# Reading out a bank of the main products ahead of the weights and the other side tasks

## The chip, the cores and the metric

The kernel runs on one core of one Trainium2 chip. The metric is the device time of one execution in microseconds. Shown is the median of several runs; beside them stands one execution that the hardware profiler recorded.

## The reference

A two-layer encoder trunk over 512 tokens of width 1024, in float32. Each layer normalises its input, multiplies it with one wide input projection, feeds the result to a token mixer (dilated window attention in layer 0, grouped attention with rotary positions in layer 1), to an attention into 256 memory tokens and to a gate, and projects the gated heads back:

```python
for i in range(DEPTH):
    h = rmsnorm(x, norm_g[i])
    mem_h = rmsnorm(mem, mem_norm_g[i])
    proj = jnp.einsum('bsd,de->bse', h, w_in)          # w_in_a[0] or w_in_b[0]
    ...
    o_mem = memory_attention(q_mem, mem_h, w_mem_kv[i], mem_qn_g[i], mem_kn_g[i])
    y = jnp.concatenate([o_mix, o_mem], axis=-1) * jax.nn.silu(gate)
    x = x + jnp.einsum('bse,ed->bsd', y, w_out[i])
```

## The kernel before

**Exact products in three passes.** Every float32 operand is split into a high part that TensorE takes and a low rest. `mm3` (L147 to L149) issues high x high, high x low, low x high. For the activations the split is made once. For the weights it is made on the way, per tile of 128 x 1024: ScalarE copies the loaded tile `wl` into the high part `wh` (L262), VectorE subtracts it to get the low part `wo` (L272). Both have rings of four buffers.

**Seven products for eight.** A projection is cut into chunks of columns, and each chunk into two by two blocks. `s_chunk` computes it with seven block products in the order of `PRODUCTS`: 12, 11, S1, S2, S4, S3, 22. The sums of weight blocks that this needs are made by VectorE (L231) and by accumulating DMAs that POOL issues (L236, L241, L246). Products with the flag `fresh` begin a new bank of PSUM (`pj`, four banks); S2, S4 and S3 go on in a bank that an earlier product left, after it was read out. Two kinds of generators read the banks: `keep` (ScalarE, L334) copies a bank to SBUF (`sn`), and `add` (VectorE, L344) adds a bank to such a copy, or subtracts, and then goes on with the consumer `ev` of that chunk: norms (L495, L385, L386, L500), rotary positions, transposes, or the gate.

**Slots.** The order of instructions is written by hand, there is no scheduler. After each group of matmuls (a slot) `s_chunk` calls three things in this order: `W.advance()`, which traces at most one `wo` (L272), one sum of weights, one `wh` (L262) and the loads (L217) and forces what the next slot needs; then, if the product is complete, `drv.spawn(f(...), d)` for the generators that read it; then `drv.tick()`, which advances every generator of the queue `urgent` that is due, then those of `bulk` (the attention pipelines), and last the functions of `after`, such as the low parts of transposed probabilities (`lo`, L636 and L1308). With `d` of 2 or 3 a readout is traced one or two slots behind the end of its product, behind that slot's `wo`, sum and `wh`, and at its place among the other generators.

A chunk of layer 0's heads (`head_chunk`) has 512 columns per block, two banks per product and two slots per product; the chunks of layer 1 and the gates have 256, one bank and one slot. The sequence is: a chunk for the values of layer 0, the keys and values of the memory (`mem_kv`, through the plainer `chunk`), eight heads and three gate chunks of layer 0, the output projection (`out_proj`, with operands `y` that `prep_y` makes at L736, L752 to L762), then the same for layer 1, whose attention (`attn_b`: `sb`, `pb`, `ptb`, `pbT`, `ob`) and memory attention (`mem_attn`: `sm`, `pm`, `pmt`, `pmT`, `om`) run as pipelines between the slots.

Of the kernel before, what the change touches and what calls it, by code (L numbers as in the profile page):

```python
# [39 lines left out]
class Driver:  # L40
# [5 lines left out]
    def __init__(self):  # L46
        self.slot = 0
        self.urgent = []
        self.bulk = []
        self.after = []  # L50
        self.first = []

    def spawn(self, gen, delay=0):
        self.urgent.append([self.slot + delay, gen])
# [46 lines left out]
        self.after = []  # L101

    def drain(self):
        while self.urgent or self.bulk or self.first:
            self.tick(ACTIVE)


# [1 line left out]
def trunk_kernel(ctx: ExitStack, tc: tile.TileContext, x, mem, wall, norm_g, mem_norm_g, gcol,  # L109
# [9 lines left out]
    drv = Driver()  # L119
# [7 lines left out]
    def s2(dt=F32, name="s2"):  # L127
        return pool.tile([128, 512], dt, tag="s2", name=name, bufs=NS2)

    def pj(name="pj"):  # L130
        return psum.tile([128, 512], F32, tag="pj", name=name, bufs=4)
# [14 lines left out]
    def mm3(o, lh, ll, rh, rl, start, stop):  # L146
        T.matmul(o, lh, rh, start=start, stop=False, skip_group_check=True)  # L147
        T.matmul(o, lh, rl, start=False, stop=False, skip_group_check=True)  # L148
        T.matmul(o, ll, rh, start=False, stop=stop, skip_group_check=True)  # L149
# [156 lines left out]
    def chunk(units, nb, group, evac):  # L306

        ps = [None] * nb
        for u in range(units):
            w = []  # L310
            for h, l in (W.take(), W.take()):
                w += [(h[:, k * 512:(k + 1) * 512], l[:, k * 512:(k + 1) * 512]) for k in range(2)]
            for b in range(nb):
                if u == 0:
                    ps[b] = pj()
                group(w, u, b, ps[b])
                W.advance()
                if u == units - 1:
                    drv.spawn(evac(b, ps[b]), 2)
                drv.tick()  # L320
# [5 lines left out]
    def s_chunk(n, act, ev, tokens=True, pre=None, half=False):  # L326


        units, per = n // 256, 1024 // n
        bank, snap = [None, None], {}  # L330

        def keep(name, u, b):
            t = snap[name, u] = s2(name="sn")
            A.copy(t, b)  # L334
            yield 1
            if name == "s3":
                c = snap["s5", u]
                V.tensor_tensor(c, c, t, ALU.subtract)
                yield 1
                yield from ev("22", u, c)  # L340

        def add(q, name, u, b):
            t = snap[name, u]
            V.tensor_tensor(t, b, t, ALU.subtract if q == "12" else ALU.add)  # L344
            yield 1
            yield from ev(q, u, t)

        after = ((keep, "z"), (add, "11", "z"), (keep, "s5"), (keep, "s2"), (add, "12", "s2"), (keep, "s3"), (add, "21", "s3"))
        for i, (a, s, fresh) in enumerate(PRODUCTS):
            while a not in act:  # L350
                drv.tick()
            if fresh:
                bank[s] = [pj() for _ in range(units)]
            for x in range(units):
                wh, wo = [t.rearrange("p (k c) -> p k c", c=n) for t in W.take()]
                ah, al = act[a][:, 0], act[a][:, 1]
                for b in range(2):
                    if pre and i == x == 0 and b:
                        pre()
                    if half and b:  # L360
                        n_half[0] += 1
                        if n_half[0] % half == 0:
                            drv.half()
                    o = bank[s][b] if units == 2 else bank[s][0][:, b * 256:(b + 1) * 256]
                    bs = slice(b * 128, (b + 1) * 128)
                    for k in range(per):
                        kk = x * per + k
                        st, sp = fresh and kk == 0 and (units == 2 or b == 0), kk == 3
                        if tokens:
                            mm3(o, ah[:, kk, bs], al[:, kk, bs], wh[:, k], wo[:, k], st, sp)  # L370
                        else:
                            mm3(o, wh[:, k, bs], wo[:, k, bs], ah[:, kk], al[:, kk], st, sp)
                W.advance()
                if x == units - 1:
                    f, *arg = after[i]
                    for u in range(units):
                        d = 2 if f is keep else 2 + u + (units == 1 and i == 6)
                        drv.spawn(f(*arg, u, bank[s][u]), d)
                drv.tick()

    def rstd_of(ss, n):
# [69 lines left out]
    def proj_t(act, sels, evac):  # L451

        def group(w, u, b, p):
            for k in range(4):
                kk = 4 * u + k
                mm3(p, sels[b](act, 0, kk), sels[b](act, 1, kk), w[k][0], w[k][1], kk == 0, kk == 7)
        chunk(2, len(sels), group, evac)
# [200 lines left out]
    def out_rest(ys, acc, done, evac):  # L658

        for n in range(2):  # L660
            def group(w, u, b, p):
                cs = slice(b * 128, (b + 1) * 128)
                while any(y is None for y in ys):
                    drv.tick()
                for k in range(4):
                    mm3(p, ys[k][0][:, cs], ys[k][1][:, cs], w[k][0], w[k][1], k == 0, k == 3)

            def ev(b, p, n=n):
                V.tensor_tensor(acc[b][n], p, acc[b][n], ALU.add)
                yield 1  # L670
                while (n, b) not in done:
                    yield 1
                yield from evac(n, b, acc[b])
            chunk(1, 4, group, ev)


    def gates(od, o_done):
# [3 lines left out]
        def gate(H, first, g, half=False):  # L681
# [6 lines left out]
            def ev(q, u, t):  # L688
# [29 lines left out]
                if {(2, 0, j), (2, 1, j)} <= y_done:  # L718
                    for k in range(2):
                        ys[2 * j + k] = (yt[j][0][:, k], yt[j][1][:, k])  # L720

            s_chunk(256, H, ev, tokens=False, half=half)

        def prep_y():
# [45 lines left out]
    def out_proj(YW, ys, src, evac, tiles, half=False):  # L770

        acc, done = {}, set()

        def load():
            for i in range(2):
                for u, t in enumerate(tiles()):
                    nc.sync.dma_start(t, src[2 * i + u])
                    acc[2 * i + u] = halves(t)
                yield 2

        def ev(q, u, t):
            b, n = 2 * (int(q[0]) - 1) + u, int(q[1]) - 1
            while b not in acc:
                yield 1
            V.tensor_tensor(acc[b][n], t, acc[b][n], ALU.add)
            done.add((n, b))

        drv.spawn(load(), ACC_AT)
        s_chunk(512, YW, ev, half=half)
        out_rest(ys, acc, done, evac)  # L790
# [89 lines left out]

    drv.spawn(mem_norm(0), MEM_AT)
    s_chunk(512, H, ev_v0, pre=second)
    km, vm = mem_kv(0, Ms[0])

# [582 lines left out]
```

## Time and profile before

| | us |
|---|---|
| median of 3 runs (lowest to highest) | 1008.05 (1007.2 to 1014.04) |
| the profiled execution | 1009.92 |
| its span, first to last instruction | 1008.1 |
| TensorE matmuls busy | 961.4 (95%) |
| VectorE busy | 831.5 (82%) |
| ScalarE busy | 644.1 (64%) |
| POOL busy | 331.2 (33%) |

In the profile PE is TensorE, DVE VectorE, ACT ScalarE, POOL GpSimd, SP the queue that issues most loads; L272 is line 272 of the kernel before. A row of the timeline has the start in us, the length in us, the engine, the line, the operation, what it writes and reads, and in brackets how long the engine was idle before it and what ended that. The chain that ended last runs for 55% of the span over TensorE and for 16% over VectorE. The mean granted clock of TensorE is 0.985.

### The profile page before, as it was taken

The numbers are of one execution on the slowest core, as the hardware profiler recorded it, in microseconds if no ns is written. First come the engines' busy times: TensorE is split into PE (matmuls) and PEld (weight loads), VectorE is DVE, ScalarE is ACT, GpSimd is POOL, SyncE is SP. The second block draws the span as 40 slices with busy tenths as digits, with TensorE's granted clock in tenths as the row PEclk, the third lists the DMA queues.
The fourth block names the chain that finished last, engine by engine and source line by source line (L and its number), as shares of the span: only waits on it lengthen the run. The fifth ranks groups of instructions, "written<-read, shape, count | busy, mean of one in ns | idle before, by whom it ended". The sixth has DMA issues, their size and how long they took to land.

```text
span 1008.1 us, 16611 instructions
## 1 busy us (share of the span) xinstructions
PE 961.4 (95%) x5724; PEld 845.4 (84%) x5724; DVE 831.5 (82%) x1496; ACT 644.1 (64%) x1623; POOL 331.2 (33%) x461
## 2 busy tenths in 40 slices
PE   7999999999999999999999889998999889998998
PEld 4779888887878787878899878887999888987886
DVE  6787688778787878787879898979789898889975
ACT  4556578686767676767776665566667566557650
POOL 1223325564545454545552010132631320001000
PEclk9999999999999999999999999999999999999899
DMA  8969936959685858686859593689565745755432
GB/s 337 289 215 353 267 88 174 311 113 263 143 256 143 254 146 252 146 252 155 229 159 312 158 278 134 235 319 271 128 145 144 197 110 173 187 174 139 133 125 84
DMA packets 85670, 201.41 MB, mean 200 GB/s; under 512 B 24913, under 2 KB 35665, under 8 KB 85586
## 3 DMA queue, kind: packets, MB, share of 16 engines
q1 hardware_dynamic: 70034, 146.28, 41.3%
q0 software_dynamic: 14256, 51.91, 27.0%
q10 hardware_dynamic: 1296, 2.16, 0.6%
q8 instruction: 45, 0.74, 0.3%
q14 instruction: 39, 0.32, 0.1%
HBM read 153.07 MB, written 12.65 MB: 164 GB/s over the span
## 4 chain that ended last, share of the span: by engine, by line
PE 55%; DVE 16%; issue 3%; DMA 3%; ACT 2%; POOL 0%; SPq 0%; DVEq 0%; ACTq 0%
PE pj L147 14%; PE pj L148 14%; PE pj L149 14%; DVE wo L272 4%; DVE wl L231 2%; PE oo L1097 1%; PE pt L1076 1%; PE qT L507 1%; DMA oth<-ds 1%; PE sa L995 1%; DVE sn L344 1%; PE ptb L1299 1%; DVE yS L736 1%; PE ob L148 1%; PE ob L149 1%
## 5 line engine op out<-in xcount | busy, mean ns | idle before, releaser
L272 DVE TENSOR_TENSOR wo<-wl,wh 128x1024 fp32r<-128x1024 f32 x255 | 316.6, 1244 | 8.7 <-ACT wh L262 8.6
L262 ACT CAST wh<-wl 128x1024 fp32r<-128x1024 f32 x255 | 267.6, 1056 | 39.9 <-PE pj L149 21.8
L147 PE MATMUL pj<-wh,hS 128*128 128x512 f32 (+1 forms) x448 | 166.4, 371 | 6.2 <-DVE sn L344 6.2
L148 PE MATMUL pj<-wo,hS 128*128 128x512 f32 (+1 forms) x448 | 159.8, 357 | 3.0 <-DVE wo L272 2.9
L149 PE MATMUL pj<-wh,hS 128*128 128x512 f32 (+1 forms) x448 | 159.8, 357 | 0.0
L148 PE MATMUL pj<-wo,h 128*128 128x512 f32 (+1 forms) x336 | 120.2, 358 | 6.3 <-DVE wo L272 6.3
L147 PE MATMUL pj<-wh,h 128*128 128x512 f32 (+1 forms) x336 | 124.0, 369 | 1.6 <-ACT h L141 1.6
L149 PE MATMUL pj<-wh,h 128*128 128x512 f32 (+1 forms) x336 | 119.8, 356 | 0.0
L386 POOL TENSOR_TENSOR rstd<-mse,half 128x4 f32<-128x4 f32 (+2 forms) x98 | 104.5, 1066 | 8.2
L147 PEld LDWEIGHTS pj<-wh,hS 128*128 128x128 f32 x448 | 86.4, 193 | 16.9 <-DVE sn L344 6.9
L148 PEld LDWEIGHTS pj<-wo,hS 128*128 128x128 f32 x448 | 86.6, 193 | 14.3 <-DVE wo L272 4.5
L149 PEld LDWEIGHTS pj<-wh,hS 128*128 128x128 f32 x448 | 86.2, 192 | 12.1
L495 ACT ACTIVATE junk<-sn 128x128 f32<-128x128 f32 x264 | 78.9, 304 | 23.1 <-DVE sn L344 20.6
L385 POOL TENSOR_SCALAR mse<-hss 128x4 f32<-128x4 f32 (+1 forms) x86 | 51.2, 595 | 114.9 <-ACT junk L495 110.4
L334 ACT COPY sn<-pj 128x512 f32<-128x512 f32 x132 | 72.3, 583 | 9.3 <-PE pj L149 9.3
L148 PEld LDWEIGHTS pj<-wo,h 128*128 128x128 f32 x336 | 64.5, 192 | 16.3 <-DVE wo L272 8.9
L246 POOL DMA_DIRECT2D wl<-wl x33 | 29.6, 898 | 142.4 <-DVE wo L272 88.5
L939 POOL TENSOR_TENSOR ta<-sn,tabs 128x128 f32<-128x128 f32 (+1 forms) x64 | 36.5, 571 | 110.2 <-DVE sn L500 77.4
L147 PEld LDWEIGHTS pj<-wh,h 128*128 128x128 f32 x336 | 64.4, 192 | 9.3 <-ACT h L141 2.0
L149 PEld LDWEIGHTS pj<-wh,h 128*128 128x128 f32 x336 | 64.2, 191 | 9.0 <-DVE h L144 0.2
L344 DVE TENSOR_TENSOR sn<-pj,sn 128x512 f32<-128x512 f32 x99 | 67.7, 684 | 3.9 <-PE pj L149 3.9
L147 PE MATMUL pj<-hS,wh 128*128 128x256 f32 x192 | 58.4, 304 | 11.3 <-DVE sn L344 8.7
(225 smaller groups left out, 2457.2 us busy)
## 6 DMA issues: line engine op xcount, KB each, us to landing
wl<-in_wall_dram SPq DMA_DIRECT2D x222, 512.0 KB, 7.1
wl<-wl POOLq DMA_DIRECT2D x66, 512.0 KB, 5.4
wl<-in_wall_dram POOLq DMA_DIRECT2D x33, 512.0 KB, 8.8
od<-o SPq DMA_DIRECT2D x12, 256.0 KB, 4.8
og<-od SPq DMA_DIRECT2D x12, 256.0 KB, 7.0
odb<-o SPq DMA_DIRECT2D x12, 256.0 KB, 2.1
og<-odb SPq DMA_DIRECT2D x12, 256.0 KB, 3.5
x<-in_x_dram SPq DMA_DIRECT2D x4, 512.0 KB, 6.7
```

What stands on the lines that cost most here:

```text
L147: T.matmul(o, lh, rh, start=start, stop=False, skip_group_check=True)
L148: T.matmul(o, lh, rl, start=False, stop=False, skip_group_check=True)
L149: T.matmul(o, ll, rh, start=False, stop=stop, skip_group_check=True)
L246: G.dma_start(self.tile[key], self.tile[c, "T2", x], accum_op=ALU.add)
L262: A.copy(wh, self.tile[self.items[i]])
L272: V.tensor_tensor(wo, self.tile[key], wh.bitcast(F32), ALU.subtract)
L334: A.copy(t, b)
L344: V.tensor_tensor(t, b, t, ALU.subtract if q == "12" else ALU.add)
L385: G.tensor_scalar(e, ss, EPS, None, ALU.add)
L386: G.tensor_tensor(r, e, half[:, 0:n], ALU.pow)
L495: A.activation(jk, p[:, j * 128:(j + 1) * 128], AF.Square, scale=QS, accum_out=ss[:, j:j + 1])
L939: G.tensor_tensor(ta[:, 0:n], xn[:, 0:n, 0:32], ropeA[:, 0, b, s0:s0 + n], ALU.mult)
```

## The change

`Driver` gets a third kind of queue, `banks`. The generators that read out a bank are no longer put into `urgent` with `spawn`, but into `banks` with `release`, with the same delay. `free()` is called directly behind each group of matmuls, in front of `W.advance()`: it takes the first step of every generator whose delay ends with this slot, so the readout itself is traced there, and then appends the generator to the end of `urgent` for its further steps. The slot of a readout stays the same; within the slot it comes before the `wo`, the sum, the `wh`, the loads and the other generators. As the generators enter `urgent` later than before, their further steps can also come behind those of others.

```diff
+        self.banks = []
+
+    def release(self, gen, delay):
+
+        self.banks.append([self.slot + delay, gen])
+
+    def free(self):
+        due = [t for t in self.banks if t[0] <= self.slot + 1]
+        self.banks = [t for t in self.banks if t[0] > self.slot + 1]
+        for _, gen in due:
+            try:
+                self.urgent.append([self.slot + 1 + max(1, next(gen)), gen])
+            except StopIteration:
+                pass
...
     def drain(self):
-        while self.urgent or self.bulk or self.first:
+        while self.urgent or self.bulk or self.first or self.banks:
+            self.free()
             self.tick(ACTIVE)
...
                 group(w, u, b, ps[b])
+                drv.free()
                 W.advance()
...
+                drv.free()
                 W.advance()
                 if x == units - 1:
                     f, *arg = after[i]
                     for u in range(units):
                         d = 2 if f is keep else 2 + u + (units == 1 and i == 6)
-                        drv.spawn(f(*arg, u, bank[s][u]), d)
+                        drv.release(f(*arg, u, bank[s][u]), d)
                 drv.tick()
```

## The prediction

> **What bounds the kernel now.** I read the page first, for the share of each engine.
>
> ```profile
> PE 961.4 (95%) x5724; PEld 845.4 (84%) x5724; DVE 831.5 (82%) x1496; ACT 644.1 (64%) x1623; POOL 331.2 (33%) x461
> ```
>
> TensorE works 961.4 us of a span of 1008.1 us, so 46.7 us is all that any new order of the other engines can fill, apart from matmuls that run at a lower clock. VectorE, at 82%, is the next. The average hides where TensorE waits, so the waits of TensorE come next, taken by stage: the start (0 to 66 us), the heads of layer 0 (240 to 500), the end of layer 0 (500 to 612) and layer 1 (700 to the end). A row gives waiter and releaser, then total us, times, and the longest.
>
> ```profile
> PE pj L148 <- DVE wo L272: 4.1, 4, 2.0
> ```
> ```profile
> PE pj L148 <- DVE wo L272: 4.0, 5, 1.0
> ```
> ```profile
> PE pj L147 <- DVE sn L344: 3.7, 2, 2.7
> PE pj L148 <- DVE wo L272: 2.0, 3, 1.5
> ```
> ```profile
> PE pj L147 <- DVE sn L344: 15.6, 7, 3.4
> PE pj L147 <- ACT sn L334: 1.8, 1, 1.8
> ```
>
> Two different bounds show. In layer 0 TensorE waits for weights (`wo`, the low part that VectorE makes at L272) and, in the heads, never for a readout of a bank. In layer 1 it is the other way round: 15.6 us of waits for L344, the readout `sn<-pj` on VectorE, and no wait for `wo` among them. The change moves readouts in front of weights, so it takes from the one and gives to the other.
>
> The timeline of TensorE in layer 1 shows the five long waits (start us, length, engine, line, operands; in brackets the idle time before and what ended it).
>
> ```profile
> 704.28 0.38 PE L147 MATMUL pj<-wh,hS 128*128 128x256 f32 x1 [2.30 <-DVE sn L344]
> ...
> 786.95 0.39 PE L147 MATMUL pj<-wh,hS 128*128 128x256 f32 x1 [3.28 <-DVE sn L344]
> ...
> 817.71 0.39 PE L147 MATMUL pj<-hS,wh 128*128 128x256 f32 x1 [3.19 <-DVE sn L344]
> ...
> 856.60 0.39 PE L147 MATMUL pj<-hS,wh 128*128 128x256 f32 x1 [2.36 <-DVE sn L344]
> ...
> 932.41 0.80 PE L147 MATMUL pj<-wh,y 128*128 128x512 f32 x1 [3.36 <-DVE sn L344]
> ```
>
> They cost more than their length. The view by stretches gives the granted clock (the column after POOL) behind three of them, and the load of the engines (busy us of TensorE, its weight loads, VectorE, ScalarE, POOL) in three longer stretches.
>
> ```profile
> 570.00:609.00 39.00, 33.22 (x191) 29.21 (x190) 37.90 (x62) 23.75 (x37) 5.26 (x6) 0.91 0.93 251
> 704.20:709.30 5.10, 5.02 (x29) 5.03 (x30) 4.08 (x3) 2.47 (x10) 5.10 (x3) 0.67 0.31 106
> 786.90:791.20 4.30, 4.25 (x23) 4.25 (x24) 4.23 (x8) 1.75 (x9) 2.73 (x3) 0.60 0.93 221
> 700.00:904.00 204.00, 191.43 (x1500) 186.26 (x1499) 176.73 (x284) 127.57 (x320) 51.45 (x52) 0.97 0.59 157
> 904.00:940.00 36.00, 30.35 (x176) 26.41 (x176) 33.99 (x58) 23.61 (x47) 3.50 (x4) 0.91 0.56 133
> 932.40:938.00 5.60, 5.59 (x17) 4.77 (x18) 5.53 (x11) 2.27 (x5) 0.00 (x0) 0.51 0.43 86
> ```
>
> After the wait at 704.28 TensorE runs 5.1 us at a clock of 0.67 and so loses 5.1 x 0.33 = 1.7 us; after 786.95 it loses 4.3 x 0.40 = 1.7, after 932.41 5.6 x 0.49 = 2.7. [...]
>
> **The change, part by part.** No instruction is added or removed. In the two built programs the queues of POOL and SP are the same line for line, and TensorE's too but for one place where four transposes are split, so no DMA moves in its queue. What moves lies on VectorE and ScalarE: 95 of the 99 readouts L344 go ahead of one `wo` L272 (often also of `wl` L231 and the normalising steps of that slot), and the snapshot copies L334 go ahead of one `wh` L262. A readout already came one slot behind its product, so it seldom waits itself.
>
> *What it costs: the heads.* The pattern at the end of one head, VectorE and then TensorE:
>
> ```profile
> 450.19 1.22 DVE L272 TENSOR_TENSOR wo<-wl,wh 128x1024 fp32r<-128x1024 f32 x1
> ...
> 451.60 0.68 DVE L344 TENSOR_TENSOR sn<-pj,sn 128x512 f32<-128x512 f32 x1
> ```
> ```profile
> 451.46 0.50 PE L148 MATMUL pj<-wo,h 128*128 128x512 f32 x1 [0.73 <-DVE wo L272]
> ```
>
> The `wo` ends at 451.41 and TensorE, already waiting, uses it at 451.46: 0.05 us of slack. In the new order the readout at 451.60 stands in front. VectorE starts one instruction behind a readout 0.60 us after it (786.21 and 786.81 in a fence below), so this wait grows by 0.60. There are five in the heads (4.0 us, 5 times): 3.0 us. Nothing hides it: that row was the only wait of TensorE in the 260 us, so it has no later wait in a head in which a delay could vanish.
>
> *What it costs: the start.* Here there are four waits for `wo`, of which the change touches three. Two of the rows, and the copies that go in front on ScalarE:
>
> ```profile
> 35.92 0.50 PE L148 MATMUL pj<-wo,hS 128*128 128x512 f32 x1 [1.05 <-DVE wo L272]
> ...
> 50.98 0.51 PE L148 MATMUL pj<-wo,hS 128*128 128x512 f32 x1 [0.76 <-DVE wo L272]
> ```
> ```profile
> 50.80 1.06 ACT L334 COPY sn<-pj 128x512 f32<-128x512 f32 x2
> ```
>
> Twice a readout goes ahead of the awaited `wo` (0.6 each); once, at 50.98, the two copies go ahead of the `wh` from which it is made (1.0). That is 2.2; I take 2.0. Costs together: 5.0 us, at least 0 if idle time of VectorE ahead of these places absorbs it, at most 8 if three more `wh` of layer 0, each held back 1.0 by the two copies, come late too.
>
> *What it brings: none at the end of layer 0.* The 3.7 us of waits for L344 and the 2.0 for `wo` in 500 to 612 look like a gain. But VectorE is busy 37.90 of the 39 us, its work there is the same in either order, and the first weights behind it start TensorE's next full stretch. The bound is a gain of 1.1 (its whole idle time) and a loss of 1.2 (two more readouts in front); I take 0.
>
> *What it brings: layer 1.* Around 786.95, VectorE:
>
> ```profile
> 781.34 1.22 DVE L272 TENSOR_TENSOR wo<-wl,wh 128x1024 fp32r<-128x1024 f32 x1
> ...
> 786.21 0.69 DVE L344 TENSOR_TENSOR sn<-pj,sn 128x512 f32<-128x512 f32 x1
> 786.81 0.16 DVE L619 RECIPROCAL rdm<-denm 128x2 f32<-128x2 f32 x1
> ...
> 787.53 0.69 DVE L636 TENSOR_TENSOR pmT<-pmt,pmT 128x512 fp32r<-128x512 f32 x1
> ```
> ```profile
> 791.78 0.36 PE L147 MATMUL om<-pmT,vm 128*128 128x256 f32 x1
> ```
>
> The readout at 786.21 moves up to 781.34, 4.87 us, more than the wait of 3.28, which goes away. With the clock 5.0 us are wanted. VectorE, however, has the same work and no idle time here, so what is late next is `pmT` of L636: it ends at 788.22 and TensorE now uses it at 791.78. TensorE can come 3.6 us earlier, not more. That is the pattern for the rest: wait plus clock is wanted, and the slack of the next tight result, plus idle time of VectorE that closes up on the way, is the cap.
>
> At 817.71, wanted 3.19 + 1.7 = 4.9. Next late is `pbT` L1308, 1.80 ahead of its use, and 1.01 of idle time can go: cap 2.8.
>
> ```profile
> 823.52 0.69 DVE L1280 TENSOR_REDUCE nmb<-sb 128x1 f32<-128x512 f32 x1 [1.01 <-PE sb L149]
> ...
> 829.40 0.68 DVE L1308 TENSOR_TENSOR pbT<-ptb,pbT 128x512 fp32r<-128x512 f32 x1
> ```
> ```profile
> 831.88 0.28 PE L148 MATMUL ob<-pbT,vb 128*128 128x256 f32 x1
> ```
>
> At 856.60, wanted 2.36. Next late is `pbT` again, 0.61 ahead, with 1.10 of idle time: cap 1.7.
>
> ```profile
> 862.96 0.69 DVE L1308 TENSOR_TENSOR pbT<-ptb,pbT 128x512 fp32r<-128x512 f32 x1 [1.10 <-ACT pbT L1303]
> ...
> 867.09 0.68 DVE L1308 TENSOR_TENSOR pbT<-ptb,pbT 128x512 fp32r<-128x512 f32 x1
> ```
> ```profile
> 868.38 0.28 PE L148 MATMUL ob<-pbT,vb 128*128 128x256 f32 x1
> ```
>
> At 704.28, wanted 2.30 + 1.7 = 4.0; VectorE and ScalarE idle soon after it, and I find no cap: 4.0. From 890 on, the wait on ScalarE (1.8), the one at 932.41 (3.36) and its clock (2.7) want 7.9, but VectorE is busy 33.99 of 36 us, and `pbT` stands 2.48 ahead of its use:
>
> ```profile
> 933.46 0.68 DVE L1308 TENSOR_TENSOR pbT<-ptb,pbT 128x512 fp32r<-128x512 f32 x1
> ```
> ```profile
> 936.62 0.42 PE L148 MATMUL ob<-pbT,vb 128*128 128x256 f32 x1
> ```
>
> I take 2.1, as a new wait there can cost clock again. Gains: 4.0 + 3.6 + 2.8 + 1.7 + 2.1 = 14.2 us. Bounds: 6 if each cap is met at half, 25 if none binds (15.6 + 1.8 + clock of about 8).
>
> *Sum:* 14.2 - 5.0 = 9.2 us less. The profiled execution took 1009.92 us (span 1008.1, 1.8 around it), so 1000.7 like for like. It lies 1.9 above the median of the runs shown (1008.05), so the median goes to 998.8.
>
> **The rivals.** *The caps do not bind* (pipelines of attention re-time themselves, since ScalarE and VectorE follow TensorE): 25 - 5 = 20 less, 988. For it: VectorE idles 27 us from 700 to 904 (busy 176.73 of 204), which by itself is enough. Against: most of it lies behind the tight results, not ahead.
>
> *The stall moves* (VectorE becomes the bound of layer 1): gains of 6, costs of 5, 1007. For it: 904 to 940, where VectorE is full. Against: its idle time between the five waits.
>
> *Head of line, the slower side.* A readout that reaches VectorE before its product ends holds the weights behind it:
>
> ```profile
> 92.24 1.22 DVE L272 TENSOR_TENSOR wo<-wl,wh 128x1024 fp32r<-128x1024 f32 x1
> 95.71 0.69 DVE L344 TENSOR_TENSOR sn<-pj,sn 128x512 f32<-128x512 f32 x1 [2.26 <-PE pj L149]
> ```
>
> Now `wo` at 92.24 fills time in which the readout could not run; in the new order it starts at 96.3, and VectorE is 1.2 us further behind. If each of the eleven chunks of layer 0 paid that, 13 us, with costs of 5 and gains of 6: 12 more, 1020. It decides once a weight's slack is under 1.2 us plus the hold; here it is not, as `wo` is first used at 98.44:
>
> ```profile
> 98.44 0.28 PE L148 MATMUL pj<-wo,hS 128*128 128x256 f32 x1
> ```
>
> [...]
>
> *The change doesn't act*: where both orders end in the same last wait, gains of 5 meet costs of 5: 1008.
>
> **How the numbers follow.** This kernel's measurement can tell about 1%, 10 us, from no change. Forecast (995 to 1003) 0.45, the line of 998 inside it: 0.20 faster by over 1%, 0.25 within. Caps that do not bind 0.20, faster. Stall moves 0.18 and no action 0.04, within. Head of line 0.13, slower. Faster 0.40, within 1% 0.47, slower 0.13. The range of 8 in 10 reaches from the unbound caps, 987, to 1011, past the moved stall with the costs at their upper bound; it leaves out head of line and a little below.
>
> **What would show it.** In the profile after: waits of TensorE on L344 from 700 on down from 15.6 to under 4, with clocks of 1.00 near 705 and 790; new waits on `pbT` L1308 or `pmT` L636 of 1 to 3 us each; the waits for `wo` in 240 to 500 up from 4.0 to about 7; the stretch 570 to 609 as long as before. The forecast is wrong if waits on L344 stay, if waits for `wo` show in 66 to 240, or if ScalarE's `wh` becomes a releaser of TensorE.

## The result and the profile after

| | before | after |
|---|---|---|
| median of the runs (lowest to highest), us | 1008.25 (1005.79 to 1014.04) | 1001.61 (1001.16 to 1002.93) |
| profiled execution, us | 1009.92 | 1001.16 |
| its span, us | 1008.1 | 999.4 |
| mean granted clock of TensorE | 0.985 | 0.993 |

The ratio of after to before is 0.9928, with an interval of [0.9908, 0.9949]: 7.3 us less, within 5.1 and 9.3 (the two medians lie 6.6 apart). That is clear of no change, and smaller than the 1% that the prediction took as the least this measurement can tell. The prediction had 998.8 and a range of 987 to 1011. The two profiled executions differ by 8.76 us, where 9.2 was forecast.

The line numbers of the kernel after are 15 to 17 higher than before: L162 to L164 are the three matmuls of `mm3` (L147 to L149 before), L246 is the sum of weights on VectorE (L231), L287 is the low part `wo` (L272 before), L277 the high part `wh` (L262), L350 the snapshot copy of ScalarE (L334), L360 the readout on VectorE (L344), L653 and L1325 the low parts of transposed probabilities `pmT` and `pbT` (L636 and L1308). First the busy time of the engines, from the page of the kernel after.

```profile
PE 958.5 (96%) x5724; PEld 839.5 (84%) x5724; DVE 830.1 (83%) x1496; ACT 643.5 (64%) x1623; POOL 338.1 (34%) x461
```

The waits of TensorE in the kernel after, from 700 us to the end (waiter and releaser; total us, times, longest).

```profile
PE ob L163 <- DVE pbT L1325: 5.7, 5, 2.2
PE om L163 <- DVE pmT L653: 1.2, 1, 1.2
PE ptb L1316 <- DVE pbT L1325: 1.2, 1, 1.2
PE pj L164 <- DVE y L733: 0.9, 1, 0.9
...
PE pj L162 <- ACT sn L350: 0.3, 1, 0.3
```

The 15.6 us of waits for VectorE's readout are gone, and the view names L360 nowhere behind 700. In their place stand the two results that the prediction named as next late. The same view for the start (0 to 66), the heads (240 to 500) and the end of layer 0 (500 to 612):

```profile
PE pj L163 <- DVE wo L287: 4.7, 4, 1.9
...
PE pj L162 <- ACT wh L277: 1.1, 1, 1.1
```
```profile
PE pj L163 <- DVE wo L287: 5.5, 6, 1.0
```
```profile
PE pj L163 <- DVE wo L287: 5.1, 2, 4.1
PE pj L164 <- DVE wo L287: 1.2, 3, 0.7
```

At the end of layer 0 the readout is no longer named either, but the time is only renamed: 3.7 for L344 and 2.0 for `wo` before, 6.3 for `wo` now. Single places, from TensorE's timeline of the kernel after:

```profile
35.70 0.50 PE L163 MATMUL pj<-wo,hS 128*128 128x512 f32 x1 [1.67 <-DVE wo L287]
...
50.82 0.50 PE L162 MATMUL pj<-wh,hS 128*128 128x512 f32 x1 [1.13 <-ACT wh L277]
...
302.37 0.50 PE L163 MATMUL pj<-wo,h 128*128 128x512 f32 x1 [1.02 <-DVE wo L287]
...
455.62 0.50 PE L163 MATMUL pj<-wo,h 128*128 128x512 f32 x1 [1.04 <-DVE wo L287]
...
789.36 0.39 PE L163 MATMUL om<-pmT,vm 128*128 128x256 f32 x1 [1.18 <-DVE pmT L653]
...
927.41 0.39 PE L163 MATMUL ob<-pbT,vb 128*128 128x256 f32 x1 [2.23 <-DVE pbT L1325]
```

And VectorE around the wait that stood at 786.95 before. The readout now comes directly behind `pmT` and ahead of `wo`, sum and rotary steps; the next `pmT` comes at the end of the same row of work, and TensorE waits for it (789.36 above).

```profile
782.43 0.68 DVE L360 TENSOR_TENSOR sn<-pj,sn 128x512 f32<-128x512 f32 x1
783.02 1.22 DVE L287 TENSOR_TENSOR wo<-wl,wh 128x1024 fp32r<-128x1024 f32 x1
784.16 1.22 DVE L246 TENSOR_TENSOR wl<-wl 128x1024 f32<-128x1024 f32 x1
...
788.62 0.68 DVE L653 TENSOR_TENSOR pmT<-pmt,pmT 128x512 fp32r<-128x512 f32 x1
```

Four stretches of the kernel after, which answer to 570 to 609, 704.2, 786.9 and 904 to 940 of before (us, then busy us of TensorE, its weight loads, VectorE, ScalarE, POOL; then the granted clock):

```profile
574.00:613.00 39.00, 32.05 (x188) 27.45 (x186) 37.82 (x63) 22.94 (x36) 5.21 (x6) 0.96 0.93 253
708.90:714.00 5.10, 5.10 (x45) 5.10 (x44) 4.70 (x4) 3.08 (x7) 5.02 (x3) 1.00 0.31 103
787.90:792.20 4.30, 3.12 (x27) 2.93 (x26) 4.23 (x9) 2.54 (x8) 1.76 (x3) 1.00 0.96 247
...
899.00:935.00 36.00, 31.96 (x186) 28.16 (x185) 35.75 (x62) 25.90 (x51) 3.49 (x4) 0.95 0.62 149
```

The clock is 1.00 where it had been 0.67 and 0.60. In the last of the four VectorE is still fuller than before (35.75 of 36 us, 33.99 before).

**The same matmul in every trace.** To see where time went I looked up one and the same matmul at six places of each timeline and took the difference to before. The table gives what each stage added (+) or took away, in us, for the kernel after and for seven of the experiments below. The places stand at 8.5, 90.0, 249.6, 500.0, 678.1 and 983.9 us before; the last column sums from the span's start.

| | start | to 250 | heads | end of layer 0 | layer 1 | at 983.9 |
|---|---|---|---|---|---|---|
| after | +2.5 | -0.9 | +2.4 | +0.5 | -13.4 | -8.8 |
| layer 1 only | -0.6 | -0.4 | -0.1 | 0.0 | -12.5 | -13.5 |
| layer 0 only | +1.6 | +0.1 | +2.4 | +0.7 | +0.2 | +5.1 |
| readouts of VectorE only | -1.8 | 0.0 | +2.4 | -0.6 | -8.9 | -8.6 |
| behind the weights | -1.9 | -1.8 | 0.0 | +0.1 | -8.9 | -12.2 |
| behind in layer 0, in front in layer 1 | -2.9 | -1.7 | -0.1 | +0.1 | -13.2 | -17.7 |
| behind the low part | -0.8 | -1.7 | 0.0 | +0.2 | -12.1 | -14.5 |
| layer 1 only, pipelines first | -1.6 | -0.7 | -0.1 | 0.0 | | |

The second and the last row have the order of before on every engine up to about 695 us, and yet their start is 0.6 and 1.6 us shorter. So differences of up to 1.6 in the start say nothing. From 250 to 678 us rows of the same order agree within 0.2, in layer 1 within 0.9. The last row ends with a changed order of matmuls, so its last places are left open.

### The profile page after: what moved, and what is told of

It is laid out like the page before. It is cut to its first block, busy times and chain, and to the rows that moved or that the text cites. A ratio compares the mean times of both kernels' runs of the same rounds, so it can differ in the third digit from the quotient of the medians.

```text
span 999.4 us, 16578 instructions
## 1 busy us (share of the span) xinstructions
PE 958.5 (96%) x5724; PEld 839.5 (84%) x5724; DVE 830.1 (83%) x1496; ACT 643.5 (64%) x1623; POOL 338.1 (34%) x461
## 4 chain that ended last, share of the span: by engine, by line
PE 43%; DVE 23%; issue 5%; DMA 3%; ACT 2%; POOL 1%; SPq 0%; DVEq 0%; POOLq 0%; ACTq 0%
PE pj L163 11%; PE pj L164 11%; PE pj L162 11%; DVE wo L287 7%; DVE wl L246 2%; DVE sn L360 2%; PE oo L1114 1%; PE pt L1093 1%; PE qT L524 1%; DMA wl<-wl 1%; PE sa L1012 1%; DVE nmb L1297 1%; DMA oth<-ds 1%; DVE pbT L1325 1%; DVE sn L517 1%
## 5 line engine op out<-in xcount | busy, mean ns | idle before, releaser
L287 DVE TENSOR_TENSOR wo<-wl,wh 128x1024 fp32r<-128x1024 f32 x255 | 311.7, 1226 | 10.3 <-ACT wh L277 10.0
L277 ACT CAST wh<-wl 128x1024 fp32r<-128x1024 f32 x255 | 267.8, 1059 | 30.0 <-PE pj L164 11.7
L162 PE MATMUL pj<-wh,hS 128*128 128x512 f32 (+1 forms) x448 | 165.0, 368 | 1.4 <-ACT wh L277 1.1
L164 PE MATMUL pj<-wh,hS 128*128 128x512 f32 (+1 forms) x448 | 158.8, 354 | 0.0
L162 PE MATMUL pj<-wh,h 128*128 128x512 f32 (+1 forms) x336 | 123.8, 369 | 0.7 <-ACT h L156 0.7
L164 PE MATMUL pj<-wh,h 128*128 128x512 f32 (+1 forms) x336 | 119.6, 356 | 0.0
L403 POOL TENSOR_TENSOR rstd<-mse,half 128x4 f32<-128x4 f32 (+2 forms) x98 | 108.6, 1108 | 8.2
L164 PEld LDWEIGHTS pj<-wh,hS 128*128 128x128 f32 x448 | 85.0, 190 | 12.0
L162 PEld LDWEIGHTS pj<-wh,hS 128*128 128x128 f32 x448 | 85.1, 190 | 11.9 <-ACT wh L277 1.6
L350 ACT COPY sn<-pj 128x512 f32<-128x512 f32 x132 | 73.7, 590 | 27.2 <-PE pj L164 27.2
L402 POOL TENSOR_SCALAR mse<-hss 128x4 f32<-128x4 f32 (+1 forms) x86 | 48.1, 559 | 114.9 <-ACT junk L512 111.1
L956 POOL TENSOR_TENSOR ta<-sn,tabs 128x128 f32<-128x128 f32 (+1 forms) x64 | 39.6, 621 | 106.5 <-DVE sn L517 75.3
L261 POOL DMA_DIRECT2D wl<-wl x33 | 29.7, 904 | 131.6 <-DVE wo L287 86.4
L164 PEld LDWEIGHTS pj<-wh,h 128*128 128x128 f32 x336 | 64.2, 191 | 9.0 <-DVE h L159 0.2
L162 PEld LDWEIGHTS pj<-wh,h 128*128 128x128 f32 x336 | 64.2, 191 | 8.4 <-ACT h L156 1.1
L360 DVE TENSOR_TENSOR sn<-pj,sn 128x512 f32<-128x512 f32 x99 | 67.4, 684 | 4.2 <-PE pj L164 4.0
L251 POOL DMA_DIRECT2D wl<-wl x33 | 30.4, 932 | 84.1 <-DVE wl L246 34.9
```

Of the source, the lines that this page charges most:

```text
L251: G.dma_start(self.tile[key], self.tile[c, "T1", x], accum_op=ALU.add)
L277: A.copy(wh, self.tile[self.items[i]])
L287: V.tensor_tensor(wo, self.tile[key], wh.bitcast(F32), ALU.subtract)
L402: G.tensor_scalar(e, ss, EPS, None, ALU.add)
L403: G.tensor_tensor(r, e, half[:, 0:n], ALU.pow)
L956: G.tensor_tensor(ta[:, 0:n], xn[:, 0:n, 0:32], ropeA[:, 0, b, s0:s0 + n], ALU.mult)
```

## The experiments

**1. Only layer 1.** A switch chooses between the old and the new place, and is turned on at the start of layer 1.

```diff
+        self.ahead = False
...
-                        drv.release(f(*arg, u, bank[s][u]), d)
+                        (drv.release if drv.ahead else drv.spawn)(f(*arg, u, bank[s][u]), d)
...
+    drv.ahead = True
     km, vm = mem_kv(1, Ms[1])
```

> The readouts go ahead only from the memory's keys and values of layer 1 on; layer 0 keeps the old order. Theory (costs and gains are separate and add up): TensorE passes the places that stood at 61.59, 249.57, 451.46 and 678.11 us before at those times again, within 0.4 us, and then gains the same 13.4 us as the changed kernel did behind 680: span 994.8, median 997.0, ratio to before 0.989. Rival (part of the gain of layer 1 is only time that layer 0 had lost and that its later stages give back, since VectorE reaches layer 1 with the same work done): the gain behind 680 shrinks by the 4.6 us that are no longer lost ahead of it, to about 9, and the median stays at 1001 to 1002.

Measured: 995.34 us, ratio 0.988 [0.9864, 0.9895], profiled span 994.7. TensorE passes layer 0 as before and gains 12.5 us in layer 1, where the rival gave about 9. The costs of layer 0 and the gains of layer 1 are separate. The waits of TensorE from 700 on:

```profile
PE ob L164 <- DVE pbT L1327: 6.4, 5, 3.0
PE pj L165 <- DVE y L734: 1.3, 1, 1.3
PE om L164 <- DVE pmT L654: 1.2, 1, 1.2
PE ptb L1318 <- DVE pbT L1327: 1.2, 1, 1.2
```

**2. Only layer 0.** The same switch, on at first and off from layer 1 on.

> The readouts go ahead only in layer 0, up to its output projection; layer 1 keeps the old order. Theory (they add up): 4.6 us lost by 678 us as in the changed kernel, nothing won behind it, waits of TensorE on the readout of 15 to 16 us from 700 on as before: median 1012.9, ratio 1.0046. Rival (lost time is given back in layer 1): median 1008 to 1009, ratio 1.000.

Measured: 1014.53 us, ratio 1.0067 [1.0054, 1.0081]. That is 1.6 above the forecast of the theory, and the rival is out: nothing of the lost time comes back, and the old waits stand in layer 1 (TensorE from 700 on).

```profile
PE pj L163 <- DVE sn L361: 15.6, 7, 3.4
PE pj L163 <- ACT sn L351: 1.8, 1, 1.8
```

**3. Only the readouts of VectorE.** The snapshot copies of ScalarE keep the old place.

```diff
-                        drv.release(f(*arg, u, bank[s][u]), d)
+                        (drv.spawn if f is keep else drv.release)(f(*arg, u, bank[s][u]), d)
```

> Only the readouts of VectorE go ahead; the snapshot copies of ScalarE keep their old place. Theory (the readouts of VectorE carry gain and cost): the wait for the high part of a weight at 50.8 us (1.1) is gone, the heads lose 0.6 us each as in the changed kernel, and layer 1 gains 12 to 14: median 1000 to 1002. Rival (the copies on ScalarE carry the gain, since each readout of VectorE needs a copy that ScalarE made before): median 1007 to 1010, and waits on VectorE's readout of over 8 us stay from 700 on.

Measured: 1001.71 us, ratio 0.9949 [0.9934, 0.9963]. The time is what the theory said, its split isn't. The heads cost 2.4 as in the kernel after, so VectorE's readouts make that cost. The start is 4.3 us shorter than after's, 2.7 more than executions of one order differ by, and the wait for `wh` at 50.8 is gone: most of what the start had cost hung on the copies. And layer 1 gains 8.9, not 12 to 14; the missing 4 stand in new waits for the copies (TensorE from 700 on). At one place alone, 728.86, a wait of 2.47 and the half clock behind it lose 4.2 us.

```profile
PE pj L162 <- ACT sn L350: 4.3, 2, 2.5
PE ob L163 <- DVE pbT L1325: 3.5, 3, 2.4
```

**4. Behind the weights, in front of the other side tasks.** `free()` and `W.advance()` change places, in both loops.

```diff
-                drv.free()
                 W.advance()
+                drv.free()
```

> The readouts are taken behind the weights of their slot, and still in front of the other side tasks. In the five long waits of before the readout stood behind a low part and a sum of weights (2.27 us together) and then behind side tasks of 0.13 (at 704), 2.60 (787), 3.74 (818), 0.61 (857) and 3.60 us (932). Theory (the side tasks are the larger part of what held the readouts): of these waits 0.1 + 2.6 + 3.2 + 0.6 + 3.4 = 9.9 of 14.5 us go, and none of layer 0's costs of 4.6 arise: a gain of 6 to 9, median 999 to 1002, waits on the readout from 700 on of about 5 us. Rival (the weights held them): the waits on the readout stay over 11 us and the median is 1005 to 1008.

Measured: 996.92 us, ratio 0.9897 [0.9882, 0.9912], faster than with the readouts in front of the weights and 2 us below the range of the theory. Layer 0 pays nothing: the heads are as before, 3.7 us of waits for `wo`. Layer 1 gains 8.9, the upper end of what the theory gave. So of the 13 us of layer 1 about 9 come from passing the other side tasks, and the weights are worth the rest. Nearly all of that rest, 3.9 us, is the one place of 704.28 before, with its wait and 1.5 us of clock behind it. What is left of the waits from 700 on:

```profile
PE ob L163 <- DVE pbT L1325: 5.7, 4, 3.0
PE pj L162 <- DVE sn L360: 3.2, 3, 1.8
PE pj L162 <- DVE grB L1191: 2.3, 1, 2.3
```

The two lower rows, 5.5 us, are the "about 5" of the theory. The third is one place: TensorE starts at 700.91 after 2.25 us, with the matmul that waited at 704.28 for the readout before. VectorE reads out a bank here too, and the view names the small instruction behind it, which ended last.

```profile
697.82 1.21 DVE L287 TENSOR_TENSOR wo<-wl,wh 128x1024 fp32r<-128x1024 f32 x1
698.95 1.22 DVE L246 TENSOR_TENSOR wl<-wl 128x1024 f32<-128x1024 f32 x1
700.09 0.68 DVE L360 TENSOR_TENSOR sn<-pj,sn 128x512 f32<-128x512 f32 x1
700.69 0.21 DVE L1191 TENSOR_SCALAR grB<-grB 128x128 f32<-128x128 f32 x1
```

**5. Behind the weights in layer 0, in front in layer 1.** The switch stands in both loops; one is shown.

```diff
+        self.front = False
...
-                drv.free()
+                if drv.front:
+                    drv.free()
                 W.advance()
+                if not drv.front:
+                    drv.free()
...
+    drv.front = True
     km, vm = mem_kv(1, Ms[1])
```

> Layer 0 takes the readouts behind the weights of their slot, layer 1 (from the memory's keys and values on) in front of them. Theory (the two layers want different places, and what each brings adds up): 3.6 us are won by 678 us as with the place behind the weights, 12.9 behind it as with the changed order in layer 1 alone: 16.5 us less than the profiled run of before, median 991 to 992, ratio 0.984. Rival (layer 1 gains less when TensorE reaches it earlier, since VectorE's work per time grows): the 12.9 shrink by the 3.6, median 994 to 996, no better than the changed order in layer 1 alone.

Measured: 993.27 us, ratio 0.9851 [0.9831, 0.987], the lowest median of all. The two parts add up: 4.6 us by 500 and 13.2 in layer 1 in the profiled execution (span 990.4); 2.9 of the 4.6 lie in the start, where up to 1.6 says nothing. The median lies between the two ranges, 1.3 above the theory's and 0.7 below the rival's; the gain of layer 1 did not shrink, so the rival's reason is out. The waits from 700 on are those of the first experiment within 0.7.

**6. One place for both layers: behind the low part only.** `free()` is called inside `W.advance()`, between `wo` and the sum of weights.

```diff
                 self.lo()
+            drv.free()
             self.sum()
             self.hi()
...
-                drv.free()
                 W.advance()
```

> One place for both layers: behind the low part of a weight, in front of the sum of weights, the high part, the loads and the side tasks. Theory (a readout costs layer 0 only where it stands in front of an awaited low part; the sum is never awaited so soon): waits for the low part in 240 to 500 us stay at 4.0, the wait for the high part at 50.8 us (1.1) is there again since the copies stand in front of it, and layer 1 wins 11 to 12: median 994 to 996. Rival (the low part is also what holds the readouts in layer 1, 1.13 us each): waits on the readout of over 4 us stay from 700 on and the median is that of the place behind all weights, 997, or more.

Measured: 996.44 us, ratio 0.9884 [0.9866, 0.9902], 0.4 us above the range of the theory. In layer 1 this place wins 12.1 of the 13, so what held the readouts among the weights was the sum of weights and, for the copies, the `wh`, not the `wo`: the waits on the readout there are down to 1.6.

```profile
PE ob L163 <- DVE pbT L1324: 5.9, 4, 3.0
PE pj L162 <- DVE sn L360: 1.6, 2, 1.0
```

The heads cost nothing, and the wait for `wh` in the start is back at 1.1, as forecast. The median is no better than in the fourth experiment, though the span is 2.3 us shorter; the intervals overlap, so the runs don't rank these two.

**7. The pipelines first.** As the first experiment; in layer 1 `tick` advances `bulk` and the low parts of `after` ahead of `urgent`. `_readers` holds the loop over `urgent` that is taken out here.

```diff
-        for t in list(self.urgent):
-            if t[0] <= self.slot:
-                self._step(self.urgent, t)
+        if not self.pipes:
+            self._readers()
...
         for f in self.after:
             f()
         self.after = []
+        if self.pipes:
+            self._readers()
+            for f in self.after:
+                f()
+            self.after = []
```

> As the changed order in layer 1 alone, and in layer 1 the attention pipelines, with the low parts of their transposed probabilities, are traced in front of the further steps of the readouts (norms, rotary positions, gates) instead of behind them. Theory (what capped the gain is that these low parts come late on VectorE): the waits for them from 700 on, 6.4 + 1.2 + 1.2 + 0.5 = 9.3 us with the changed order in layer 1 alone, fall under 4, nothing else takes their place, and the median goes from 995.3 to 989 to 991. Rival (VectorE is full there, so what is put behind is late instead): new waits on the rotary positions, the gates or the operands of the output projection of as many us, median 994 to 998. Second rival (the low part now holds VectorE while it waits for its transposes): waits on the readouts and weights come back, median over 998.

Measured: 997.19 us, ratio 0.9891 [0.9867, 0.9916], the same as the first experiment's 0.988. The waits for `pbT` and `pmT` do fall, from 9.3 to 4.4, and others come up (TensorE from 700 on):

```profile
PE ob L174 <- DVE pbT L1338: 4.4, 2, 3.1
PE qT L1226 <- DVE sn L1266: 1.7, 2, 1.1
PE pmt L658 <- DVE qb L1276: 1.6, 1, 1.6
PE pj L174 <- DVE wo L298: 1.4, 1, 1.4
PE ptb L1329 <- DVE qb L1276: 1.3, 1, 1.3
PE pj L175 <- DVE y L744: 1.3, 1, 1.3
```

The rotated queries (`sn`, `qb`) and a `wo` are late instead, 6.0 us of waits; the wait for `y` stood in the first experiment too. All listed waits of TensorE from 700 on come to 11.7 us, against 11.4 there. The first rival holds: what is put back on VectorE is late in its turn.

**8. The fifth and the seventh together.** Layer 0 behind the weights, layer 1 in front, pipelines first.

> Layer 0 with the readouts behind the weights, layer 1 with the readouts in front and the pipelines ahead of the readouts' further steps. Theory (all three add up): 991.5 less what the pipelines bring (4 to 6): median 986 to 988. Rival (VectorE is full in layer 1): as with the two places alone, 991 to 996.

Measured: 995.05 us, ratio 0.9866 [0.9844, 0.9887]; the same as the fifth within the intervals, as the rival said. The pipelines bring nothing here either.

## Why the prediction was right, and where its steps were off

**Layer 1 (forecast -14.2, measured -13.4).** The five steps, each between places of the timeline that the change does not reorder: at 704 -3.9 (forecast 4.0), at 787 -3.6 (3.6), at 818 -2.2 (2.8), at 857 -1.6 (1.7), from 890 on -2.4 (2.1); between the first two +0.3. The caps came out, and the results they named are the ones that TensorE now waits for, with 1 to 2 us each. Waits and clock both count in the gain: behind 700 us the listed waits of TensorE fall from 19.1 to 10.2 us, and between the places 678.1 and 983.9 the clock is halved for 17.1 us before and for 3.4 after, which is worth up to 6.8 us. Taking the named results out of the way (experiment 7) gains nothing, though: another result of VectorE is late as soon as these are not, so the cap is not the place of one instruction. The rival "caps do not bind" is out. The reason that fits is the one that the rival "the stall moves" gave, VectorE's work as a whole, but it isn't shown: from 704 to 904 VectorE is busy 181 of 200 us in the kernel after, so it isn't full all through. The 6 us that this rival allowed were less than half of the gain.

**What carried it was named too narrowly.** The prediction's argument is "readouts in front of weights". Experiments 4 and 6 split the 13 us: about 9 for passing the other side tasks, 3 more for passing the sum and the high part, and 0.4 to 1.3 for passing `wo`, which is about as much as rows of one order differ by. My own rows had it (at 786.21 the readout had stood behind 2.6 us of rotary steps besides 2.3 of weights), and I didn't ask which of the two was worth more. The costs of layer 0, though, come only from the weights. That is why the place behind them beats the change. The prediction also gave the copies of ScalarE no gain beyond 890, the wait of 1.8; experiment 3 puts 4 us on them. One thing no run separates: with `release` the further steps of a readout also come later in `urgent` than with `spawn`, and what that alone brings or costs stays open.

**The heads (forecast +3.0, five times 0.60).** Between the rows at 302.37 and 455.62 three heads take 153.25 us, against 151.42 between 300.04 and 451.46: 0.61 for each. The four full heads of the table give 2.4, and the fifth place, at 249.57, adds 0.5: 2.9 us in all. The sign I had named was off: the waits in this stage rose from 4.0 to 5.5, not to 7, since only half of the 0.61 lies in the listed wait (0.73 to 1.04). The other half lies at an earlier low part of the same head, in front of which another readout now stands:

```profile
448.94 0.69 DVE L360 TENSOR_TENSOR sn<-pj,sn 128x512 f32<-128x512 f32 x1
449.55 1.21 DVE L287 TENSOR_TENSOR wo<-wl,wh 128x1024 fp32r<-128x1024 f32 x1
```
```profile
450.17 0.58 PE L162 MATMUL pj<-wh,hS 128*128 128x512 f32 x1
450.81 0.50 PE L163 MATMUL pj<-wo,hS 128*128 128x512 f32 x1
```

The low part ends at 450.76, TensorE starts with it at 450.81, and the two matmuls stand 0.64 apart instead of 0.42 (446.61 and 447.03 before). A stall of 0.2 us doesn't make a row in the view of waits.

**The start (forecast +2.0, measured +2.5).** The sum came near, the parts did not. The matmul that waited 1.05 at 35.92 before waits 1.67 now (35.70 above): 0.6 for one readout in front of a `wo`. The second readout that I priced, in front of the `wo` of 61.59, costs nothing; the wait is 0.33 in both kernels. The two copies in front of a `wh` cost 1.3 where I had 1.0 (the wait of 1.13 at 50.82). Behind that wait the clock is halved, which costs 1.6 more and was not in my sum, and at 10 us TensorE waits 0.9 less for `h`, where nothing was moved. That the half clock isn't the price of the order is shown by experiment 6: the same wait of 1.13 for `wh` stands there, and the 20 matmuls behind it run at full clock. The first row is of the kernel after, the second of experiment 6, between the same two matmuls.

```profile
53.10:57.87 4.77, 4.77 (x20) 3.84 (x18) 3.11 (x5) 0.94 (x2) 1.73 (x2) 0.64 0.22 43
```
```profile
50.99:54.16 3.17, 3.17 (x20) 2.70 (x18) 2.71 (x5) 0.94 (x2) 1.72 (x2) 1.00 0.38 75
```

So a clock fall that I had left out and a luckier wait about cancel each other in the 2.5. I also listed `wh` as a releaser among the things that would prove the forecast wrong, and had priced just that in the sum: the sign was badly chosen.

**The end of layer 0 (forecast 0, bounds -1.1 and +1.2).** Measured +0.5 over the stage, and the stretch of 39 us holds 37.82 us of VectorE, as before 37.90. That VectorE sets the time there is shown by a pair of rows that no experiment was meant for: up to here the first experiment has the order of before, and its clock did not fall. The first two rows are of before, the others of the first experiment, at the same matmuls.

```profile
576.10:582.90 6.80, 6.08 (x28) 6.11 (x29) 6.77 (x9) 2.63 (x5) 0.89 (x1) 0.50 1.00 278
576.00:609.50 33.50, 29.57 (x159) 25.56 (x160) 32.73 (x55) 19.72 (x30) 4.40 (x5) 0.90 1.04 294
```
```profile
575.20:582.00 6.80, 6.12 (x51) 6.15 (x52) 6.76 (x9) 3.89 (x6) 0.89 (x1) 1.00 0.95 280
575.10:608.60 33.50, 27.46 (x159) 22.95 (x160) 32.72 (x55) 19.82 (x30) 4.41 (x5) 1.00 1.03 293
```

Half clock over 6.8 us, and the 159 matmuls take 33.5 us either way: VectorE is busy 32.7 of them, and the lost clock is free.

**Head of line and no action.** No wait shows in 66 to 240 after the change, so no weight there lost its slack to a readout that came too early. Both rivals are out. The sign for the first was too sharp, though: before itself has a wait of 1.1 for `wo` there, and the second experiment, with after's order in layer 0, one of 0.7.

**From the sum to the median.** 8.8 against 9.2 is the sum's error; the median is off by 2.8 (1001.6 against 998.8). I subtracted the 9.2 of one profiled execution from the median too. With more runs, before's median is 1008.25, so its profiled execution was 1.7 slow, while after's was 0.45 fast; that makes up 2.1 of the 2.8. A part of that luck is in the start, where before's execution took up to 1.6 longer than others of the same order. Another part is the clock: before's mean was 0.985 here, and 21 of 22 further executions of the same kernel, taken beside the experiments, had a higher one. Seven of them had 0.993, the value of after; their spans are 1005.0 to 1007.4, against 999.4 to 1000.6 for the four executions of after at 0.993. So about 6 us of the gain stand without a difference in the mean clock.

## What to carry to other kernels

When something is moved to the front of a queue, price separately what it passes: here the cheap part of the move (past the side tasks) brought 9 of 13 us and the dear part (past the weights) brought the costs, so a step half as far was better than the whole, and the best was the far step only in the layer where nobody waits for weights. A gain capped by the next late result is priced well by that result's slack; but removing that cap needs a look at the engine's whole load, since on VectorE the next one was waiting (experiment 7: 4.9 us of the named waits less, 6.0 us of others). And a difference taken from one pair of profiled executions carries their luck: look where the same order of instructions gives different times before putting it on a median.

## What the runs showed of the hardware

In these runs the granted clock doesn't follow the length of one gap. In layer 1 of the second experiment, whose order there is that of before, the wait at 704.28 is there again with the same 2.30 us, and the clock behind it stays up:

```profile
709.11 0.39 PE L163 MATMUL pj<-wh,hS 128*128 128x256 f32 x1 [2.30 <-DVE sn L361]
```
```profile
709.00:714.10 5.10, 4.99 (x41) 4.99 (x42) 4.87 (x4) 3.29 (x11) 5.10 (x3) 1.00 0.32 106
```

In before it was 0.67 there. TensorE's next 20 us took 1.5 us less, near the 1.7 that I had counted. So that part of a gain depends on chance, and at 787 the same execution lost 1.2 more than before did.

The records of the clock change only at multiples of 3.413 us from each other: up to 990 us the profiled execution of before shows half clock six times, four times for 3.413 us and twice for 6.827, that of after four times for 3.413. I divided the ten traces into windows of that length and took the share of each in which matmuls and transposes ran. Of 2660 windows at full clock between 60 and 980 us, the 28 with the lowest shares, up to 0.470, were each followed by half clock, and none of the others, from 0.477 up, was. In before these are five, with 0.219 to 0.453, and the next one has 0.480; in after two, with 0.237 and 0.468, and the next has 0.486. In the first 60 us it isn't as clean: in the second experiment a window with a share of 0.451 was not followed by half clock and one with 0.492 was, and near 5 us windows with 0.33 to 0.46 kept the full clock. In before the 2.30 us lay mostly in one window (share 0.45); in the second experiment they were split over two (0.54 in the emptier one). What sets the clock no run shows: these are the shares that were measured and what came behind them.
